# RWKV-7 scan on one core: initial states centred once ahead of the scan, and the copies of the masked product moved to ScalarE

## The chip, the core and the metric

The kernel runs on one core of one Trainium2 chip. The metric is the device time of the whole program in microseconds. An execution of the same kernel was also recorded by the hardware profiler; all rows below come from that record. The engines are named as in the profile: PE (TensorE's matmuls), PEld (its weight loads), DVE (VectorE), ACT (ScalarE), POOL (GpSimd) and SP (SyncE, which here only issues DMAs). A small q behind a name is the engine's own sequencer.

## The reference

One layer of a hybrid backbone. Rows of 128 context tokens and 2048 latent tokens, 1024 wide, are normalised, modulated and projected once. Half of the width goes through an RWKV-7 mixer of 8 heads of 64, scanned in both directions:

```python
def step(S, inp):
    r_t, w_t, k_t, v_t, kk_t, a_t = inp
    s_kk = jnp.einsum('bdhij,bdhj->bdhi', S, kk_t)
    S = (S * w_t[..., None, :] - s_kk[..., :, None] * (kk_t * a_t)[..., None, :]
         + v_t[..., :, None] * k_t[..., None, :])
    return S, jnp.einsum('bdhij,bdhj->bdhi', S, r_t)
s_final, ys = lax.scan(step, s0.astype(f32), xs)
y = ys[:, 0] + jnp.flip(ys[:, 1], axis=1)
mean = jnp.mean(y, axis=-1, keepdims=True)
var = jnp.mean(jnp.square(y - mean), axis=-1, keepdims=True)
y = ((y - mean) * lax.rsqrt(var + GN_EPS)).reshape(b, t, A_WIDTH)
```

For the context s0 is zero, and its final states are an output; for the latent tokens s0 is a given cached state for each direction and head. The other half is a gated three-tap convolution. Both halves are gated, joined, projected again, added to the input and normalised. The mean over the 64 values of a head that the last lines take away is linear in the state, so the kernel removes it from the values and from the initial states rather than from y.

## The kernel before

Three phases follow each other: the projections and gates (`phase1`, to about 1000 us), the scan (`phase2`, about 1000 to 1560 us) and the output projection (`phase3`). Only the scan and its entry are touched.

The scan works in 17 stages. A stage is a pair of heads p (0 to 3) and a block of 512 latent tokens (0 to 3), so p changes every four stages; one more stage, the sixteenth, does the context for all heads. Each stage has two groups, direction 0 and direction 1, and a group has 8 chunks (units) of 64 tokens. A chunk becomes matrix work:

- `partL` loads the operands rr of a stage, `partM` builds from them, three stages ahead (LA = 3), the block-diagonal bd (ACT), the masked products F and GA (matmuls psF and psG, masks by DVE at L893), the transposed Q (ACT), and writes the blocks dg to memory (scr_at, L897 to L899).
- `partI` solves the triangular systems of a stage on POOL: it loads ab, runs a long row of small operations (L931, L934) and writes zt to memory (scr_zt, L935).
- `partW` fills the two operand rings stl and str of the next stage: parts come by DMA (`load_stk`, L843 and L846), parts are copies from GA (`copy("g", ...)`, L950) and from Q (`copy("h", ...)`, L952). It also loads the values into the upper half of sv (`load_v`, L822) and zc from scr_zt (L959).
- `partU` transposes zc to zr (DVE, L965) and builds the operand zb (matmuls psU and psW, ACT copies to bu and zb). `partB` computes psX, which ACT puts into stl or str (L777), and psE, which DVE masks into E (L1011).
- `partS` walks the 8 chunks in order: psS is E times sv; its lower half, scaled by DVE (L1063), is the state in the lower half of the next chunk's sv. At the first chunk of a direction, for each p, the state is loaded from the input st0 into sv (L1042), and DVE takes away its mean with three operations on mn and sv (L1044 to L1046). In the context stage the state is set to zero by POOL instead.
- `finish` normalises y (yss, y) and writes it.

The helper `copy` (L772 to L779) chooses the engine: a copy goes to DVE when its letter is in `ON_DVE`, which holds the letter g alone, and to ACT otherwise. All plain copies therefore have line L779, on both engines, and are told apart by their tiles. The order of instructions on each engine comes from a scheduler that plays the whole program through with modelled costs; each engine then runs its row in that order, and an instruction that waits holds all that stand behind it on the same engine. DMAs are issued by SP, except scr_at (ACT) and scr_zt (POOL).

Of the kernel before, what the change touches and what calls it, by code (L numbers as in the profile page):

```python
# [6 lines left out]
F32 = mybir.dt.float32  # L7
# [3 lines left out]
ALU = mybir.AluOpType  # L11
# [668 lines left out]

NST = 17
MORD = ("Ff", "GgD", "", "Q")
ON_DVE = "g"
LA = 3


# [4 lines left out]
def phase2(K):  # L691
    nc, tc, A, S = K.nc, K.tc, K.A, K.S
    V, G, P, T = nc.vector, nc.gpsimd, nc.scalar, nc.tensor
    D = nc.sync.dma_start
    MF, MG, ME = (0, 1), (0, 1), (2, 3)
    B = Ctx()
    O = Ctx()
    O.scaled = None

    def setup_first():  # L700

        O.r0 = Pool(K, "p2r0", "right")
        O.rI = Pool(K, "p2rI", "right")
        O.r1 = Pool(K, "p2r1", "right")
        O.pm = Pool(K, "p2m", "right", 2, PSUM)
        B.msk = O.r0.tile([128, 4, 128], F32, name="msk")
        B.mkg = O.r0.tile([128, 2, 128], F32, name="mkg")
        for i, j in enumerate((0, 2, 4, 5)):
            D(B.msk[:, i], A["msk"][:, j, 0:128])
        for i, j in enumerate((1, 3)):  # L710
            D(B.mkg[:, i], A["msk"][:, j, 64:192])
        B.I2 = O.r0.tile([128, 64], F32, name="I2")
        D(B.I2[:], A["i2"])
        B.idt = O.r0.tile([128, 128], F32, name="idt2")
# [45 lines left out]
    def ring(pool, n, shape, name, init=None):  # L760
        l = [pool.tile(shape, F32, name=f"{name}{i}") for i in range(n)]
        if init:
            for t_ in l:
                init(t_)
        st = [0]

        def get():
            st[0] += 1
            return l[(st[0] - 1) % n]
        return get  # L770

    def copy(k, dst, src, negate=False):  # L772
        if negate:
            if k in ON_DVE:
                V.tensor_scalar(dst, src, -1.0, None, ALU.mult)
            else:
                P.activation(dst, src, AF.Copy, scale=-1.0)  # L777
        else:
            (V.tensor_copy if k in ON_DVE else P.copy)(dst, src)  # L779

# [15 lines left out]
    def tl(shape, tag, b, pool=None, dt=F32):  # L796
        return (pool or O.l0).tile(shape, dt, tag=tag, name=f"{tag}_{K.u()}", bufs=b)
# [21 lines left out]
    def load_v(dst, units):  # L819
        if units[0][0] == units[-1][0]:  # L820
            p, c0 = units[0]
            D(dst.rearrange("t u h v -> t u (h v)"), S["vt"][c0 * 64:(c0 + 8) * 64, p * 128:(p + 1) * 128].rearrange("(u t) c -> t u c", t=64))  # L822
        else:
            for u in range(2):
                D(dst.rearrange("t (g u) h v -> t u g (h v)", u=2)[:, u], S["vt"][u * 64:u * 64 + 64, :].rearrange("t (g c) -> t g c", g=4))
# [22 lines left out]
    def half(g, n):  # L848

        h = n if g.d == 0 else 1 - n  # L850
        return slice(h * 4, h * 4 + 4)
# [57 lines left out]
    def partI(s, st):  # L909
# [24 lines left out]
                G.tensor_tensor(zt[:, :kn, j + 2:32], zt[:, :kn, j + 2:32], tv[:, :, r], ALU.subtract)  # L934
        G.dma_start(S["zt"][s].rearrange("h u s b q i -> (h u s b) (q i)"), zf)  # L935

    def partW(s, st):

        for g in st.g:
            g.lt, g.rt = B.lt(), B.rt()  # L940
            g.fs, g.gs = (g.lt, g.rt) if g.d == 0 else (g.rt, g.lt)
            g.E = []
        for n in range(2):
            for g in st.g:
                us = half(g, n)
                load_stk(g.fs, g, 2, us)
                load_stk(g.gs, g, 1, us)
                for i in range(2):
                    r = slice(64 - i * 64, 128 - i * 64)
                    copy("g", g.gs[64:128, 1, i, us], g.GA[r, us, 0:64])  # L950
                    k = us.start // 2
                    copy("h", g.gs[64:128, 0, :, us.start + i:us.stop:2], g.Q[i * 64:i * 64 + 64, k:k + 2].rearrange("p k (h c) -> p h k c", h=2))  # L952
                if n == 0:
                    g.sv = tl([128, 8, 2, 64], "sv", 4)
                    load_v(g.sv[64:128], g.units)
            if n == 0:
                st.zc = tl([128, 16, 32], "zc", 1, O.l1)
                for h in range(2):
                    D(st.zc[h:128:2], S["zt"][s][h].rearrange("u s b q i -> (s b q) u i"))  # L959
            yield  # L960
# [54 lines left out]
    def partS(s, st, nxt):  # L1015

        sp = {}
        for i in range(8):
            for gi, g in enumerate(st.g):
                d = g.d  # L1020
                ctx = g.blk is None
                u = i % 4 * 2 + i // 4 if ctx else i
                u = u if d == 0 else 7 - u
                p, c = g.units[u]
                if ctx:
                    first = c == (0 if d == 0 else 1)
                    lastc = not first
                else:
                    first = c == (2 if d == 0 else 33)
                    lastc = c == (33 if d == 0 else 2)  # L1030
                sv = g.sv
                n, k = (u // 4 if d == 0 else 1 - u // 4), u % 4

                m, q = (u % 2, u // 2) if ctx else (u // 4, u % 4)
                if i == 0 and not ctx and gi in held:
                    G.tensor_copy(sv[0:64, u], held.pop(gi)[:])
                if first:
                    if ctx:
                        G.memset(sv[0:64, u], 0.0)
                    else:  # L1040
                        x = sv[0:64, u]
                        D(x, A["st0"][:, d, 2 * p:2 * p + 2, :])  # L1042
                        mn = tl([64, 2], "mn", 2)
                        V.tensor_reduce(mn[:], x, mybir.AxisListType.X, ALU.add)  # L1044
                        V.tensor_scalar(mn[:], mn[:], -1.0 / 64, None, ALU.mult)
                        V.tensor_tensor(x, x, mn[:].unsqueeze(2).broadcast_to((64, 2, 64)), ALU.add)  # L1046
                if i % 4 == 0:
                    sp[gi] = O.pS.tile([128, 4, 2, 64], F32, tag="S", name=f"psS{s}_{gi}_{i}")
                for hd in range(2):
                    T.matmul(sp[gi][:, q, hd, :], g.E[n][:, k, hd, :], sv[:, u, hd, :], start=True, stop=True)  # L1050
                if not (lastc and not ctx):
                    if ctx and lastc:
                        so = tl([64, 2, 64], "so", 2)
                        dst = so[:]
                    elif (not ctx) and i == 7:
                        if nxt.g[gi].blk is None:
                            held[gi] = tl([64, 2, 64], "held", 2)
                            dst = held[gi][:]
                        else:
                            dst = nxt.g[gi].sv[0:64, 0 if d == 0 else 7]  # L1060
                    else:
                        dst = sv[0:64, u + (1 if d == 0 else -1)]
                    r = V.tensor_tensor(dst, sp[gi][0:64, q], B.pc[0:64, d, 2 * p:2 * p + 2, c:c + 1].broadcast_to((64, 2, 64)), ALU.mult)  # L1063
                    O.scaled = r.ins
                    if ctx and lastc:
                        D(S["nst"][:, d, 2 * p:2 * p + 2, :], so[:])
                if i % 4 == 3:
                    outputs(g.units[0][0], g.blk, m, sp[gi])
            yield
# [74 lines left out]
    def first(s):  # L1144
        sts[s] = partL(s)
        yield from partM(s, sts[s])
        partI(s, sts[s])

    def early():
        setup_first()  # L1150
        for s in range(2):
            yield from first(s)

    def main():
# [64 lines left out]
        for p in (O.l0, O.rI, O.r0):  # L1219
            p.close()  # L1220

    K.early, K.main, K.spare = early, main, spare


# [14 lines left out]
    return dict(st0=st0, msk=m, i2=i2, idt=np.eye(128, dtype=np.float32))  # L1239


SCR2 = dict(at=(NST, 16, 2, 2, 32, 32), zt=(NST, 2, 16, 2, 2, 16, 32), nst=(64, 2, 8, 64))

# [128 lines left out]
def build(nc, tc, A, outs):  # L1372
# [9 lines left out]
    K.S = dict(outs)  # L1382
    for name, shape in {**SCR, **SCR2, "gate": (2, 1024)}.items():
        if name not in K.S:
# [24 lines left out]
```

## Time and profile before

| what | value |
|---|---|
| median of 3 runs | 1766.98 us (1766.21 to 1769.92) |
| the profiled execution | 1765.65 us |
| its span in the profile | 1763.5 us |
| TensorE busy in the span | 1638.5 us, 93% |
| VectorE busy | 1163.8 us, 66% |
| ScalarE busy | 815.3 us, 46% |
| GpSimd busy | 585.4 us, 33% |

The shares are means over three phases. A row of the timeline gives the start, the busy time, the engine, the line, the operation with the tiles that it writes and reads, how many instructions are merged, and in square brackets how long the engine stood idle before it and what released it. A row of waits gives the total, the number of times and the longest. A row of a group gives the busy time, the mean of one instruction in ns and the idle time before it. A row of forms gives the shortest, the median and the longest duration in ns.

### The profile page before, as it was taken

Reading aid. Unit: us, or ns where it says so; the run is one execution under the profiler, and the core shown is the slowest. Engines: PE = TensorE matmul, PEld = TensorE weight load, DVE = VectorE, ACT = ScalarE, POOL = GpSimd, SP = SyncE. Lnnn points to the kernel's source line nnn. Section 1 sums busy time; section 2 is a strip of 40 time slices with the busy share of each in tenths; the row PEclk is TensorE's granted clock in tenths of the full one; section 3 lists DMA queues with packets and bytes.
Section 4 is the critical chain, followed back from the end, with each engine's and each line's share of the span. In section 5 each row is a group of like instructions: output and inputs, shape, how many; then the busy total and the mean of one; then the engine's idle time right before and its main releaser. Section 6 shows DMA issues by size and latency. Waiting matters only on the chain. (4 is left out here: it accounts for less than half of the span.)

```text
span 1763.5 us, 33040 instructions
## 1 busy us (share of the span) xinstructions
PE 1638.5 (93%) x12400; PEld 1544.7 (88%) x12400; DVE 1163.8 (66%) x2249; ACT 815.3 (46%) x1583; POOL 585.4 (33%) x1089
## 2 busy tenths in 40 slices
PE   5999999998999998999999789899799899899998
PEld 2888889898999998999999789899799899887786
DVE  6875788866466866556773666677677777656333
ACT  4533455434144433334342367567577576533222
POOL 0011111101011111011120777767777868323221
PEclk8999999999999999999999899899999999899999
DMA  9787778785456646567767566667766875645442
GB/s 364 208 234 217 232 251 256 227 251 145 151 147 228 171 149 168 173 212 233 222 196 255 135 168 170 151 162 182 187 161 185 187 181 128 180 158 193 152 143 90
DMA packets 315664, 335.15 MB, mean 190 GB/s; under 512 B 166953, under 2 KB 263849, under 8 KB 301425
## 3 DMA queue, kind: packets, MB, share of 16 engines
q1 hardware_dynamic: 243200, 323.99, 61.5%
q10 hardware_dynamic: 70944, 4.60, 2.8%
q0 software_dynamic: 1360, 4.46, 0.7%
q8 instruction: 98, 1.61, 0.4%
q14 instruction: 62, 0.50, 0.1%
HBM read 221.16 MB, written 111.82 MB: 189 GB/s over the span
## 5 line engine op out<-in xcount | busy, mean ns | idle before, releaser
L934 POOL TENSOR_TENSOR zt<-zt,ztmp 128x30 f32<-128x30 f32 (+7 forms) x510 | 199.0, 390 | 39.1
L1010 PE MATMUL psE<-str,stl 128*128 128x128 f32 x1088 | 147.4, 280 | 13.0 <-DVE E L1011 11.1
L1050 PE MATMUL psS<-sv,E 128*128 128x64 f32 x1088 | 154.6, 274 | 2.0 <-DVE sv L1063 1.9
L1050 PEld LDWEIGHTS psS<-sv,E 128*128 128x128 f32 x1088 | 144.5, 198 | 5.2 <-DVE sv L1063 3.0
L1010 PEld LDWEIGHTS psE<-str,stl 128*128 128x128 f32 x1088 | 132.2, 193 | 15.4 <-DVE E L1011 12.0
L931 POOL TENSOR_TENSOR ztmp<-ab,zt 128x60 f32<-128x60 f32 (+7 forms) x255 | 133.1, 522 | 19.3
L779 ACT COPY bd<-rr 64x512 f32<-64x512 f32 x136 | 83.9, 617 | 84.1 <-issue 27.2
L323 POOL TENSOR_TENSOR shk<-rawl 128x384 f32<-128x384 f32 (+1 forms) x24 | 22.1, 920 | 292.3 <-ACT rawl L319 292.3
L1011 DVE TENSOR_TENSOR E<-psE,msk 128x512 f32<-128x512 f32 x136 | 93.2, 686 | 30.2 <-PE psE L1010 28.1
L1063 DVE TENSOR_TENSOR sv<-psS,pc 64x128 f32<-64x128 f32 x254 | 68.0, 277 | 42.1 <-PE psS L1050 40.4
L999 PE MATMUL psX<-F,zb 128*128 128x128 f32 x544 | 77.7, 295 | 18.5 <-DVE E L1011 17.1
L999 PEld LDWEIGHTS psX<-F,zb 128*128 128x128 f32 x544 | 70.5, 206 | 21.6 <-DVE E L1011 20.0
L892 PE MATMUL psF<-rr,bd 128*128 128x128 f32 x544 | 79.0, 291 | 9.9 <-DMA rr<-scr_ops 3.9
L1345 POOL TENSOR_TENSOR z<-z,x 128x512 f32<-128x512 f32 x32 | 43.6, 1366 | 129.1 <-DVE z L1341 107.1
L892 PE MATMUL psG<-rr,bd 128*128 128x128 f32 x544 | 73.9, 282 | 10.1 <-DVE F L893 10.1
L197 POOL TENSOR_TENSOR hslb<-kd,hshb 128x384 fp32r<-128x384 f32 (+1 forms) x24 | 26.0, 1084 | 163.7 <-ACT hshb L196 157.6
L892 PEld LDWEIGHTS psF<-rr,bd 128*128 128x128 f32 x544 | 70.3, 202 | 11.4 <-issue 6.1
L160 PE MATMUL mmc<-h,w 128*128 128x384 f32 (+1 forms) x192 | 67.5, 352 | 13.3 <-ACT q1r L321 9.7
L892 PEld LDWEIGHTS psG<-rr,bd 128*128 128x128 f32 x544 | 67.6, 196 | 10.4 <-DVE F L893 10.3
L323 POOL TENSOR_TENSOR shv<-rawl 128x384 f32<-128x384 f32 (+1 forms) x24 | 21.3, 888 | 151.9 <-ACT rawl L319 146.5
L893 DVE TENSOR_TENSOR F<-psF,msk 128x512 f32<-128x512 f32 x68 | 46.4, 683 | 30.4 <-PE psF L892 16.5
L162 PE MATMUL mmc<-h,w 128*128 128x384 f32 (+1 forms) x192 | 66.0, 344 | 0.0
(307 smaller groups left out, 5230.4 us busy)
## 6 DMA issues: line engine op xcount, KB each, us to landing
w<-scr_wsp SPq DMA_DIRECT2D x68, 1024.0 KB, 7.0
scr_wsp<-w SPq DMA_DIRECT2D x34, 1024.0 KB, 5.9
rr<-scr_ops SPq DMA_DIRECT2D x64, 512.0 KB, 4.8
scr_ops<-sp SPq DMA_DIRECT2D x160, 192.0 KB, 5.3
wr<-in_win SPq DMA_DIRECT2D x34, 512.0 KB, 6.3
ab<-scr_at SPq DMA_DIRECT2D x34, 256.0 KB, 4.1
x<-in_x SPq DMA_DIRECT2D x17, 512.0 KB, 3.8
wadas<-in_wada SPq DMA_DIRECT2D x8, 1024.0 KB, 13.0
```

What stands on the lines that cost most here:

```text
L160: T.matmul(ps[:, :n], w[:, 0, k], hh[:, 0, k, :n], start=k == 0, stop=False)
L162: T.matmul(ps[:, :n], w[:, 1, k], hh[:, 0, k, :n], start=False, stop=k == 7)
L779: (V.tensor_copy if k in ON_DVE else P.copy)(dst, src)
L892: T.matmul(ps[:, i, :].rearrange("p (a b) -> p a b", b=64), w[:, u, :], x[:, :, u, :], start=True, stop=True)
L893: V.tensor_tensor(dst[:, h * 4:h * 4 + 4, :], ps[:], mask.unsqueeze(1).broadcast_to((128, 4, 128)), ALU.mult)
L931: G.tensor_tensor(tv, ab[:, j:j + 2, j + 2:32].unsqueeze(1).broadcast_to((128, kn, 2, n)), zt[:, :kn, j:j + 2].unsqueeze(3).broadcast_to(( ...
L934: G.tensor_tensor(zt[:, :kn, j + 2:32], zt[:, :kn, j + 2:32], tv[:, :, r], ALU.subtract)
L999: T.matmul(px[:, i, :], B.zb[:, gi, us.start + i, :], g.F[:, us.start + i, :], start=True, stop=True)
L1010: T.matmul(pe[:, i, hd, :].rearrange("p (b t) -> p b t", b=2), g.lt[:, :, hd, us.start + k + i].rearrange("p b t -> p (b t)"), g.rt[:, :, ...
L1011: V.tensor_tensor(g.E[n][:, k:k + 2].rearrange("p a b c -> p (a b) c"), pe[:].rearrange("p a b c -> p (a b) c"), B.msk[:, ME[g.d]].unsquee ...
L1050: T.matmul(sp[gi][:, q, hd, :], g.E[n][:, k, hd, :], sv[:, u, hd, :], start=True, stop=True)
L1063: r = V.tensor_tensor(dst, sp[gi][0:64, q], B.pc[0:64, d, 2 * p:2 * p + 2, c:c + 1].broadcast_to((64, 2, 64)), ALU.mult)
```

## The change

The letter g leaves `ON_DVE`, so the copies of GA into stl and str, two for each half and direction of a stage, 136 of 64 x 256 in all, are made by ScalarE. The initial states of both directions and all heads are loaded once, ahead of the first stages' preparation (`center_states`, called in `early`), freed of their means by three operations of VectorE over 64 x 1024, and stored to a scratch in memory, sti. The eight loads of states into sv then read this scratch, and are issued by `partW`, directly behind the load of the values (`first_states`); `partS` no longer loads or centres. The context stage's zeros are set in `first_states` too.

```diff
--- before.py
+++ after.py
-ON_DVE = "g"
+ON_DVE = ""
...
+    def first_states(g):
+
+        for u, (p, c) in enumerate(g.units):
+            if g.blk is None and c == g.d:
+                G.memset(g.sv[0:64, u], 0.0)
+            elif g.blk is not None and c == (2 if g.d == 0 else 33):
+                D(g.sv[0:64, u], S["sti"][:, g.d, 2 * p:2 * p + 2, :])
+
+    def center_states():
+
+        x = O.rI.tile([64, 16, 64], F32, tag="ab", name="st0", bufs=2)
+        D(x[:], A["st0"].rearrange("k d h v -> k (d h) v"))
+        mn = O.rI.tile([64, 16], F32, tag="dgp", name="st0mean", bufs=1)
+        V.tensor_reduce(mn[:], x[:], mybir.AxisListType.X, ALU.add)
+        V.tensor_scalar(mn[:], mn[:], -1.0 / 64, None, ALU.mult)
+        V.tensor_tensor(x[:], x[:], mn[:].unsqueeze(2).broadcast_to((64, 16, 64)), ALU.add)
+        D(S["sti"].rearrange("k d h v -> k (d h) v"), x[:])
...
@@ partW
                 if n == 0:
                     g.sv = tl([128, 8, 2, 64], "sv", 4)
                     load_v(g.sv[64:128], g.units)
+                    first_states(g)
...
@@ partS
-                if ctx:
-                    first = c == (0 if d == 0 else 1)
-                    lastc = not first
-                else:
-                    first = c == (2 if d == 0 else 33)
-                    lastc = c == (33 if d == 0 else 2)
+                lastc = c == ((1 if d == 0 else 0) if ctx else (33 if d == 0 else 2))
...
-                if first:
-                    if ctx:
-                        G.memset(sv[0:64, u], 0.0)
-                    else:
-                        x = sv[0:64, u]
-                        D(x, A["st0"][:, d, 2 * p:2 * p + 2, :])
-                        mn = tl([64, 2], "mn", 2)
-                        V.tensor_reduce(mn[:], x, mybir.AxisListType.X, ALU.add)
-                        V.tensor_scalar(mn[:], mn[:], -1.0 / 64, None, ALU.mult)
-                        V.tensor_tensor(x, x, mn[:].unsqueeze(2).broadcast_to((64, 2, 64)), ALU.add)
...
@@ early
         setup_first()
+        center_states()
...
+SCR2: sti=(64, 2, 8, 64)
```

The scheduler orders the program anew. Instructions on PE and POOL are as many as before, DVE has 157 fewer, ACT has 136 more, and SP has two more. In the new file the masking of E is at L1030, the state's scaling at L1067, y at L1084, zr at L984 and the load of zc at L978. Late in phase 1, where PE waits for the first rr near 934 us, SP's row now has the load of the states ahead of the four loads of rr, and PE's row has eight mmgb matmuls ahead of the first psF.

The first place is VectorE's row at the start of the scan, behind the setup of the rings; F and GA are the masked products of stage 2, whose psF and psG run at that time. Before:

```order
L794 COPY str_10032<-I_9259 64x512 x2
L794 COPY str_10033<-I_9259 64x512 x2
L779 COPY str_10032<-GA_9266 64x256 x2
L779 COPY stl_10027<-GA_9269 64x4x64 x2
L893 TENSOR_TENSOR F_10011<-psF_0_0_10070,msk 128x512
L893 TENSOR_TENSOR F_10011<-psF_0_1_10076,msk 128x512
L779 COPY str_10032<-GA_9266 64x256 x2
L779 COPY stl_10027<-GA_9269 64x4x64 x2
L893 TENSOR_TENSOR GA_10012<-psG_0_0_10082,mkg 128x512
```

and after:

```order
L794 COPY str_10040<-I_9260 64x512 x2
L794 COPY str_10041<-I_9260 64x512 x2
L893 TENSOR_TENSOR F_10019<-psF_0_0_10080,msk 128x512
L893 TENSOR_TENSOR F_10019<-psF_0_1_10086,msk 128x512
L893 TENSOR_TENSOR GA_10020<-psG_0_0_10092,mkg 128x512
L893 TENSOR_TENSOR GA_10020<-psG_0_1_10098,mkg 128x512
L984 STREAM_TRANSPOSE zr_10215<-zc_10069 128x512
```

The eight copies from GA are gone from between the presets, F and GA; in ScalarE's row 16 copies, from GA and Q in turn, now stand in one piece, ahead of the next bd.

The second place is VectorE's row where stage 8 begins, the first stage of the third pair of heads (its E's, and GA of a later stage, are made there; yss and y_12550 belong to `finish`). Before:

```order
L1114 TENSOR_REDUCE yss_13276<-w_13260 128x8
L1011 TENSOR_TENSOR E_13026<-psE_0_00_13042,msk 128x512
L1063 TENSOR_TENSOR sv_12753<-psS_1_4_13008,pc 64x128
L1080 TENSOR_TENSOR y_12545<-psS_1_4_13008,y_12545 64x512
L1117 RECIPROCAL yss_13276<-yss_13276 128x8
L1044 TENSOR_REDUCE mn_13623<-sv_13150 64x2
L1011 TENSOR_TENSOR E_13034<-psE_1_00_13048,msk 128x512
L1118 TENSOR_TENSOR y_12550<-y_12550,yss_13276 128x512
L893 TENSOR_TENSOR GA_9272<-psG_0_1_13248,mkg 128x512
L1045 TENSOR_SCALAR mn_13623<-mn_13623 64x2
```

and after:

```order
L1118 TENSOR_REDUCE yss_13270<-w_13254 128x8
L1030 TENSOR_TENSOR E_13018<-psE_0_00_13034,msk 128x512
L1067 TENSOR_TENSOR sv_12745<-psS_1_4_13000,pc 64x128
L1084 TENSOR_TENSOR y_12537<-psS_1_4_13000,y_12537 64x512
L1121 RECIPROCAL yss_13270<-yss_13270 128x8
L1030 TENSOR_TENSOR E_13026<-psE_1_00_13040,msk 128x512
L1122 TENSOR_TENSOR y_12542<-y_12542,yss_13270 128x512
L893 TENSOR_TENSOR GA_9273<-psG_0_1_13242,mkg 128x512
L1030 TENSOR_TENSOR E_13018<-psE_0_01_13046,msk 128x512
L1067 TENSOR_TENSOR sv_12736<-psS_0_0_13212,pc 64x128
```

The operations on mn and sv of L1044 and L1045 are gone from between the reciprocal, the E's and y, as are the copies into str that followed; nothing here reads what a load brings into sv's lower half.

The third place is SP's row ahead of stage 3, where zc is loaded in two halves. Before:

```order
L822 DMA sv_11128<-scr_vt 64x8x128
L822 DMA sv_11137<-scr_vt 64x8x128
L868 DMA rr_9281<-scr_ops_57 128x2x512
L959 DMA zc_11139<-scr_zt 64x16x32
L846 DMA stl_10026<-scr_ops_57 64x4x64 x2
L843 DMA str_10032<-scr_ops_57 64x2x256
L843 DMA str_10033<-scr_ops_59 64x2x256
L846 DMA stl_10027<-scr_ops_59 64x4x64 x2
L959 DMA zc_11139<-scr_zt 64x16x32
```

and after:

```order
L822 DMA sv_11128<-scr_vt 64x8x128
L822 DMA sv_11137<-scr_vt 64x8x128
L978 DMA zc_11139<-scr_zt 64x16x32 x2
L846 DMA stl_10034<-scr_ops_57 64x4x64 x2
L843 DMA str_10040<-scr_ops_57 64x2x256
L843 DMA str_10041<-scr_ops_59 64x2x256
L846 DMA stl_10035<-scr_ops_59 64x4x64 x2
```

The second half of zc stood behind six loads of operands and now directly follows the first.

More of the change, by code (lines that the diff above doesn't have):

```diff
@@ L1239, in layout2 @@
     return dict(st0=st0, msk=m, i2=i2, idt=np.eye(128, dtype=np.float32))
-SCR2 = dict(at=(NST, 16, 2, 2, 32, 32), zt=(NST, 2, 16, 2, 2, 16, 32), nst=(64, 2, 8, 64))
+SCR2 = dict(at=(NST, 16, 2, 2, 32, 32), zt=(NST, 2, 16, 2, 2, 16, 32), nst=(64, 2, 8, 64), sti=(64, 2, 8, 64))
 def phase3(K):
```

## The prediction

> **What bounds the kernel now.** I read the page first, then busy time by stretches of the scan, then the waits of TensorE and VectorE, and last the timeline where a wait was long. Head of the page:
>
> ```profile
> span 1763.5 us, 33040 instructions
> PE 1638.5 (93%) x12400; PEld 1544.7 (88%) x12400; DVE 1163.8 (66%) x2249; ACT 815.3 (46%) x1583; POOL 585.4 (33%) x1089
> ```
>
> TensorE is the bound as a mean over stages, but the change touches the scan alone (about 1000 to 1560 us), so its share is to be read there. Each row is a stretch: its length, busy us of TensorE, of its weight loads, of VectorE, ScalarE and POOL (instructions in brackets), then TensorE's granted clock, the DMA share and GB/s:
>
> ```profile
> 1000.00:1050.00 50.00, 34.81 (x374) 33.20 (x373) 35.29 (x64) 29.31 (x54) 40.32 (x88) 0.86 0.67 167
> 1200.00:1250.00 50.00, 48.92 (x593) 47.93 (x592) 39.89 (x84) 37.34 (x70) 39.37 (x88) 1.00 0.78 189
> 1250.00:1300.00 50.00, 42.24 (x520) 41.49 (x519) 33.65 (x76) 27.98 (x52) 32.22 (x73) 0.93 0.67 170
> ```
>
> In a regular stretch (1200) TensorE is 98% busy at full clock: little to win there. In two others it is not: the start of the scan loses some 15 us, and 1250 to 1300 loses 8, with the clock below 1. What TensorE waits for from 1000 to 1600 us (total, times, longest):
>
> ```profile
> PE psX L999 <- DVE E L1011: 17.1, 14, 5.9
> PE psE L1010 <- DVE E L1011: 11.1, 6, 7.4
> PE psG L892 <- DVE F L893: 10.1, 1, 10.1
> PE psF L892 <- ACT Q L779: 3.5, 3, 2.7
> PE psE L1010 <- ACT stl L777: 1.7, 2, 1.3
> PE psX L999 <- ACT zb L777: 1.3, 1, 1.3
> PE psW L980 <- ACT bu L779: 1.2, 2, 0.7
> ```
>
> Some 38 us hang on VectorE, not quite 8 on ScalarE. VectorE in turn is held, in order, by one wait that the change removes:
>
> ```profile
> DVE mn L1044 <- DMA sv<-in_st: 17.1, 6, 7.7
> ```
>
> **The change, part by part.** (a) The initial states. At a change of head pair the mean's reduction stands in VectorE's row ahead of E, and its load is issued only then:
>
> ```profile
> 1265.71 0.52 SPq L1042 DMA_DIRECT2D sv<-in_st  x1
> 1269.90 0.28 DVE L1044 TENSOR_REDUCE mn<-sv 64x2 f32<-64x128 f32 x1 [7.69 <-DMA sv<-in_st]
> 1258.98 1.06 PE L1010 MATMUL psE<-str,stl 128*128 128x128 f32 x8
> 1259.87 0.56 PE L1050 MATMUL psS<-sv,E 128*128 128x64 f32 x4
> 1270.96 2.08 PE L1010 MATMUL psE<-str,stl 128*128 128x128 f32 x8 [7.40 <-DVE E L1011]
> 1272.82 0.95 PE L1050 MATMUL psS<-sv,E 128*128 128x64 f32 x4
> 1401.98 2.08 PE L999 MATMUL psX<-F,zb 128*128 128x128 f32 x8 [5.86 <-DVE E L1011]
> 1403.85 0.95 PE L1050 MATMUL psS<-sv,E 128*128 128x64 f32 x4
> 1404.60 2.02 PE L892 MATMUL psF<-rr,bd 128*128 128x128 f32 x8
> 1406.41 1.58 PE L999 MATMUL psX<-F,zb 128*128 128x128 f32 x8
> ```
>
> VectorE stands still for 7.69 us, TensorE for 7.40, and its first matmuls then run slow: 2.08 against 1.06 us for eight, 0.95 against 0.56 for four, 1.41 us in all. After the change VectorE's row holds no operation on sv here (second place of the order), and the state is wanted only by psS, whose loads now stand beside load_v in SP's queue, ahead of the stage. What is late next is the ordinary wait of psX on E: by the table above (17.1 - 5.86) / 13 = 0.86 us. First stall: 7.40 + 1.41 - 0.86 = 7.95. Second, at 1401.98: 5.86, and slow matmuls of 1.02 and 0.39 again, and, by the same pace of 1.06 for eight, 0.96 and 0.52 more, 2.89 in all; less 0.86: 7.89. Together 15.8; as bounds, nothing if another input is just as late (POOL's result, below), and 17.6 if the 0.86 goes too. What is left of VectorE's 17.1 us after these two stalls I count as nothing: it lies at the start of the scan and in stage 3, where (b) and (d) hold TensorE longer.
>
> What else this part moves: SP issues the eight state loads as before, now from scratch and directly behind load_v, which waits for the same buffer of sv; the scratch is written late in phase 1, so no new wait stands ahead of the loads of operands that follow. The context stage's eight memsets on POOL come earlier in its row and stay eight. Nothing for both; if the state loads should hold SP's queue, each holds it for its 0.52 us, 4.2 in all.
>
> (b) Start of the scan.
>
> ```profile
> 1004.51 0.59 DVE L779 COPY str<-GA 64x256 f32<-64x256 f32 x2
> 1005.12 5.62 DVE L779 COPY stl<-GA 64x256 f32<-64x256 f32 x2
> 1010.76 1.29 DVE L893 TENSOR_TENSOR F<-psF,msk 128x512 f32<-128x512 f32 x2
> 1011.51 3.68 PE L892 MATMUL psG<-rr,bd 128*128 128x128 f32 x16 [10.15 <-DVE F L893]
> 1011.81 2.50 ACT L779 COPY zb<-zc 32x512 f32<-32x512 f32 x4 [5.79 <-POOL zt L934]
> ```
>
> Four copies, of which two took 5.62 us, stand ahead of F, and TensorE waits 10.15 us for F. In the changed row F stands directly behind the presets of L794, so it could start at 1004.51: 6.25 us sooner. But zc comes no sooner than the 1011.81 at which ScalarE's zb starts, and if all waits on zc the gain is nothing. Between 0 and 6.25 I take 3.5, a little over half, because the psG that stood still needs F and not zc. ScalarE gets 16 copies in a row here, in the 5.79 us in which it was idle and a little of what lies before.
>
> (c) Late in phase 1. The row of TensorE now has eight mmgb matmuls ahead of the first psF, and SP's has center_states's load ahead of the four rr loads:
>
> ```profile
> 939.32 3.25 PE L892 MATMUL psF<-rr,bd 128*128 128x128 f32 x16 [3.95 <-DMA rr<-scr_ops]
> 944.13 0.33 PE L161 MATMUL mmgb<-h,w 128*128 128x384 f32 x1
> 944.30 0.33 PE L162 MATMUL mmgb<-h,w 128*128 128x384 f32 x1
> ```
>
> Eight at a spacing of 0.17 us fill 1.4 of the 3.95; the added load delays rr by about its issue, 0.6 us as the 0.52 above, or by more if the transfer is in the way (2.4 makes it a loss of 1). Taken: +0.8, between -1 and 1.4. The three centring operations (VectorE is 66% busy) and the store lie in this same gap, long before 1000 us: nothing; without that cover, three at 0.7 us.
>
> (d) Stage 3. The two zc loads stand apart in SP's row, with six operand loads between them, and everybody waits for the second one:
>
> ```profile
> 1104.14 0.60 SPq L959 DMA_DIRECT2D zc<-scr_zt  x1
> 1108.80 0.61 SPq L959 DMA_DIRECT2D zc<-scr_zt  x1
> 1111.60 0.71 DVE L965 STREAM_TRANSPOSE zr<-zc 128x512 f32<-128x512 f32 x1 [3.57 <-DMA zc<-scr_zt]
> ```
>
> In the new row they stand together (third place of the order): the second could go 4.66 - 0.6 = 4.1 us sooner, and VectorE's 3.57 us with it. Bounds: 0, if the POOL result is what sets it, and 9 with the stretch of slow clock behind it. Taken: 4.
>
> (e) The copies on VectorE.
>
> ```profile
> L779 ACT COPY str<-Q x68: 401/403/408, 1002.7 to 1532.2; 64x256 f32<-64x256 f32 x68
> L779 DVE COPY str<-GA x68: 286/343/1534, 1004.5 to 1531.8; 64x256 f32<-64x256 f32 x68
> L779 DVE COPY stl<-GA x68: 285/321/3547, 1005.1 to 1533.9; 64x256 f32<-64x256 f32 x68
> L779 DVE COPY stl<-GA 64x256 f32<-64x256 f32 x68 | 33.2, 488 | 1.6
> L779 DVE COPY str<-GA 64x256 f32<-64x256 f32 x68 | 31.4, 462 | 2.4 <-PE psE L1010 0.4
> ```
>
> VectorE sheds 33.2 + 31.4 = 64.6 us, ScalarE gets 136 x 0.403 = 54.8 us, 3.2 us a stage, in rows where it is 56 to 75% busy. Where the copies stand between two E's, E comes sooner. The waits on E without the two stalls are 17.1 - 5.86 + 11.1 - 7.40 = 14.9 us, of which 3 belong to the stage of (d): 11.9. Half of it, 6, is taken, since the E's also wait for psE; bounds 0 and 11.9.
>
> The Trainium skill speaks against this part: "ScalarE: Activation LUTs", section "Rules for kernel authors", has simple elementwise work go to VectorE, which is up to about three times faster there. The smallest times above (285 against 403) agree in sign, the means (488 and 462 against 403) do not: priced by the smallest, the move would add 136 x 0.12 = 16 us of work; by the means it saves 10.
>
> (f) ScalarE's side. The same copies now stand in its row ahead of zb, bu, Q and stl. TensorE's waits on it are 3.5 + 1.7 + 1.3 + 1.2 = 7.7 us. I let them grow by half, -3.7; bounds: 0, and -28 if 2 of the 3.2 us a stage come through in 14 regular stages.
>
> Sum: 15.8 + 3.5 + 0.8 + 4 + 6 - 3.7 = 26.4 us. The profiled execution took 1765.65 us (span 1763.5, the rest lies around it): 1739.25. The median of the runs is 1766.98, 1.33 more: 1740.6.
>
> **The rivals.** Part of it comes back: at the places of (a) and (d) a second input is nearly as late. For it: POOL is busy 39.37 of 50 us in the regular stretch, and in (b) and (d) ScalarE and VectorE do wait for its result or for zc. Against it: in 17 stages VectorE waited for zc only twice, and one of these is (d):
>
> ```profile
> DVE zr L965 <- DMA zc<-scr_zt: 4.2, 2, 3.6
> ```
>
> The gain is then one stall's worth and a little, 10 us: 1757.
>
> ScalarE becomes the bound, which ends on the other side. Its row is in order; if the new copies delay stl or zb, and so psE and psX, by 2.5 us in each of 14 stages, 35 us are lost against the 30.1 of the other terms: 5 us slower, 1772. It decides from 30.1 / 14 = 2.15 us a stage on. For it: in the row at 1200 it had 12.7 us in 50 free, 7.6 a stage, in pieces. Against it: it needs 3.2 of the 7.6, and TensorE waits for it 7.7 us in the whole scan. The rule of the Trainium skill on ScalarE quoted above, taken alone, points to this case.
>
> VectorE's waits vanish wholly: (e) gives 11.9, (b) 6.25, (d) 9, and (f) nothing: 15.8 + 6.25 + 0.8 + 9 + 11.9 = 43.8, or 1723; with (d) at the 4 of the sum, 38.8 and so 1728, which I take for it. For it: the copies' spread from 285 to 3547 ns while POOL works beside them, so that POOL too may gain when they leave. The Trainium skill has a reason, "SBUF — State Buffer", section "Terms": VectorE and GpSimd lock a port pair against each other, and ScalarE has its own. The 3547 ns copy, with POOL busy beside it, agrees; by that rule POOL's chain shortens too.
>
> The edit does nothing for the time: only if TensorE's 98% stretch were the whole story, which the 8 us stalls speak against.
>
> **How the numbers follow.** Forecast as summed, 1740.6: 0.45, its own range 1733 to 1750. Partly given back, 1757: 0.25. Waits vanish, 1728: 0.15. ScalarE the bound, 1772: 0.09. No change: 0.05. The last 0.01 is for what I have not thought of. A difference under 0.2% (3.5 us) cannot be told from none. Range 1726 to 1760: below it lies the part of the third case that goes to 1723, above it the last two and the upper edge of the second. Faster 0.86, same 0.05, slower 0.09.
>
> **What would show it.** Right: no VectorE wait on an sv load; TensorE's waits on E before the stages with new states under 2 us; stretch 1250 to 1300 over 46 us busy; psG's wait for F near 5; VectorE's busy time down by some 70 us and ScalarE's up by 55. Wrong: TensorE's waits on stl, zb, bu or Q growing beyond 15 us, zb or zr waiting for zc or POOL longer than before, or new waits of psS on sv<-scr_sti.

## The result, and the profile after

The changed kernel takes 1749.28 us in the median of four runs (1741.7 to 1754.7), the kernel before 1768.22 (1766.21 to 1769.92). The ratio is 0.9893, with a 95% interval of 0.987 to 0.9916: 19 us faster, where 26 were forecast. Two more comparisons on other chips gave 0.9915 (0.9885 to 0.9945) and 0.9903 (0.9868 to 0.9939). The profiled execution was one of the slower ones, at 1754.7 us. Its page begins:

```profile
span 1752.9 us, 33041 instructions
PE 1647.9 (94%) x12400; PEld 1558.8 (89%) x12400; DVE 1093.0 (62%) x2092; ACT 870.1 (50%) x1719; POOL 582.1 (33%) x1089
```

VectorE is 70.8 us less busy and ScalarE 54.8 us more, as forecast. The same stretches as before (columns as above), and what TensorE waits for in the scan:

```profile
1000.00:1050.00 50.00, 38.47 (x413) 36.26 (x412) 23.53 (x46) 32.34 (x65) 41.36 (x92) 0.97 0.76 182
1200.00:1250.00 50.00, 47.98 (x485) 46.55 (x484) 30.55 (x61) 38.28 (x73) 38.81 (x90) 0.90 0.75 177
1250.00:1300.00 50.00, 49.81 (x651) 48.81 (x650) 36.33 (x75) 39.48 (x78) 35.99 (x84) 1.00 0.76 199
```

```profile
PE psF L892 <- ACT Q L779: 9.8, 22, 1.6
PE psE L1029 <- DVE E L1030: 7.0, 4, 3.5
PE psG L892 <- DVE F L893: 4.4, 2, 4.0
PE psE L1029 <- ACT stl L777: 4.0, 4, 1.9
PE psU L992 <- DVE zr L984: 2.8, 1, 2.8
PE psX L1018 <- ACT zb L777: 2.3, 2, 1.7
```

The stretch of the old stall (1250 to 1300) is now full: 49.81 of 50 us at full clock. But 1200 to 1250, which had been full at clock 1.00, is now at 0.90. The waits on E are down from 28.2 to 7.8 us; those on ScalarE are up from 7.7 to 17.4 (with 0.7 on bu and 0.6 on bd). The row of VectorE waiting for a load of sv is gone, and another has grown:

```profile
DVE zr L984 <- DMA zc<-scr_zt: 13.9, 4, 4.8
```

Where the clock fell, in a stage with no wait over 1.5 us, TensorE's timeline reads:

```profile
1216.60 1.06 PE L892 MATMUL psF<-rr,bd 128*128 128x128 f32 x8
1217.59 1.20 PE L992 MATMUL psU<-zr,GA 32*32 32x32 f32 x64
1218.72 1.10 PE L1054 MATMUL psS<-sv,E 128*128 128x64 f32 x8
1221.28 2.08 PE L892 MATMUL psF<-rr,bd 128*128 128x128 f32 x8 [1.46 <-ACT Q L779]
1228.92 3.24 PE L1018 MATMUL psX<-F,zb 128*128 128x128 f32 x16
```

A wait of 1.46 us for Q, and for about 10 us from then on eight psF take 2.08 instead of 1.06 us, sixteen psX 3.24 instead of 1.95. The wait itself is small; the stretch at half clock behind it costs about 5 us.

For each run below the scan was split in the same way: from the first psF behind the last mmb to the end of the last psS; TensorE's idle time in it; and, in pieces of 2 us, what the granted clock lacks to 1. The rest is work at full clock. All in us, one profiled execution each:

| kernel | scan | idle | lost to the clock | rest |
|---|---|---|---|---|
| before | 598.7 | 54.0 | 25.6 | 519.1 |
| changed | 586.4 | 36.2 | 27.4 | 522.8 |
| changed, second profile | 573.2 | 29.8 | 20.5 | 522.9 |
| changed, third profile | 580.3 | 34.5 | 23.9 | 521.9 |
| states only | 585.3 | 44.7 | 20.5 | 520.1 |
| copies only | 592.6 | 42.5 | 30.7 | 519.4 |

Three executions of one program differ by 13 us in the scan, and about half of that is clock. Their mean is 580.0, 18.7 us under the kernel before: by these columns idle time is 20.5 less, clock loss 1.7 less and the rest 3.4 more. But the columns overlap where TensorE stands still at half clock: 5.8 us in the kernel before, in its three long waits, and 0.2 to 0.8 in the three. Counted once, as idle time, the clock's loss is 19.8 us before and 23.4 in the mean after, and the rest is 1.8 less. The kernel before has a single profile here. Over whole executions, the span times what the mean granted clock lacks to 1 is 55.9 us in the mean of 17 executions before and 56.5 in six of the changed kernel on one chip, 56.8 (11) and 58.6 (six) on another. The stalls went away, the lost clock did not.

### The profile page after: what moved, and what is told of

Read it like the earlier page. It is cut to its first block, busy times and chain, and to the rows that moved or that the text cites. A ratio compares the mean times of both kernels' runs of the same rounds, so it can differ in the third digit from the quotient of the medians.

```text
span 1752.9 us, 33041 instructions
## 1 busy us (share of the span) xinstructions
PE 1647.9 (94%) x12400; PEld 1558.8 (89%) x12400; DVE 1093.0 (62%) x2092; ACT 870.1 (50%) x1719; POOL 582.1 (33%) x1089
## 5 line engine op out<-in xcount | busy, mean ns | idle before, releaser
L1067 DVE TENSOR_TENSOR sv<-psS,pc 64x128 f32<-64x128 f32 x254 | 69.2, 277 | 92.9 <-PE psS L1054 92.2
L1030 DVE TENSOR_TENSOR E<-psE,msk 128x512 f32<-128x512 f32 x136 | 92.7, 684 | 33.0 <-PE psE L1029 32.3
L160 PE MATMUL mmc<-h,w 128*128 128x384 f32 (+1 forms) x192 | 67.9, 354 | 13.4 <-ACT q1r L321 9.8
L323 POOL TENSOR_TENSOR shv<-rawl 128x384 f32<-128x384 f32 (+1 forms) x24 | 25.4, 1060 | 153.4 <-ACT rawl L319 153.4
L892 PEld LDWEIGHTS psG<-rr,bd 128*128 128x128 f32 x544 | 65.7, 193 | 5.0 <-DVE F L893 4.8
L161 PE MATMUL mmc<-h,w 128*128 128x384 f32 (+1 forms) x192 | 66.1, 344 | 0.0
L162 PE MATMUL mmc<-h,w 128*128 128x384 f32 (+1 forms) x192 | 65.7, 342 | 0.0
```

The lines of the kernel that those rows point to most:

```text
L160: T.matmul(ps[:, :n], w[:, 0, k], hh[:, 0, k, :n], start=k == 0, stop=False)
L161: T.matmul(ps[:, :n], w[:, 0, k], hh[:, 1, k, :n], start=False, stop=False)
L162: T.matmul(ps[:, :n], w[:, 1, k], hh[:, 0, k, :n], start=False, stop=k == 7)
L892: T.matmul(ps[:, i, :].rearrange("p (a b) -> p a b", b=64), w[:, u, :], x[:, :, u, :], start=True, stop=True)
L1030: V.tensor_tensor(g.E[n][:, k:k + 2].rearrange("p a b c -> p (a b) c"), pe[:].rearrange("p a b c -> p (a b) c"), B.msk[:, ME[g.d]].unsquee ...
```

## The experiments

**The same kernel again.** No edit.

> The changed kernel once more, unaltered. Theory C (half-clock stretches): its times so far lie at 1741.7, 1744.3, 1754.3 and 1754.7 us, because TensorE's granted clock falls to 0.50 for some 10 us at places with short waits, not at the same places in every execution. Expected: times again spread over more than 5 us (the kernel before over less than 4), and a profile whose stretches at 0.50 lie in part at other places than 1056, 1124 and 1220 us. Rival (one fixed schedule, and the spread is a matter of the chip): times within 4 us, stretches at the same places.

Ratio 0.9915; times from 1748.7 to 1767.1, a spread of 18 us (before 1768.3 to 1781.3, 13 us, on the same chip). Two stretches at half clock of 10.2 us begin at 1127.9 and 1223.5 us (1125.7 and 1221.3 in the first profile), one of 10.2 us at 1057.4 has become one of 3.4 us at 1056.3, and the loss fell by 6.9 us. Most places recur, their length and some of them do not; the spread of before was larger than the theory said, so the comparison of spreads decides little.

**The states alone.** `ON_DVE` goes back:

```diff
-ON_DVE = ""
+ON_DVE = "g"
```

> Only the initial states are changed; the copies of GA stay on VectorE. Theory A (the states' stalls carry the gain): 14 to 18 us faster than before, TensorE waits 17.1 and 11.1 us for E fall by 13 together, no wait of VectorE for a load of sv. Rival B (the copies carry it, the stalls are refilled by the next input): under 6 us faster.

Ratio 0.9932 (0.9906 to 0.9957), that is 12 us of 1774, with an interval of 7.6 to 16.7 us. The profile has no wait of VectorE on a load of sv, and TensorE's waits on E are 8.5 and 8.2 us, 11.5 less. A little under theory A's 14 and over B's 6: the initial states carry most of the gain. One new wait has appeared, of psE for str on ScalarE (8.5 us in all, 6.3 the longest); what causes it was not followed.

**The copies alone.** In the kernel before:

```diff
-ON_DVE = "g"
+ON_DVE = ""
```

> Only the copies of GA move to ScalarE; the initial states are loaded and centred in the scan as before. Theory A: the stalls at the two changes of heads (7.40 and 5.86 us) stay, the time is within 5 us of before, since what E gains is lost to psF waiting for Q on ScalarE. Rival B: 8 us or more faster.

Ratio 0.9978 (0.9963 to 0.9993), 4 us. The stall on the states stays:

```profile
PE psE L1010 <- DVE E L1011: 14.1, 4, 6.2
PE psF L892 <- ACT Q L779: 9.1, 18, 2.1
PE psX L999 <- ACT zb L777: 6.1, 4, 1.7
DVE mn L1044 <- DMA sv<-in_st: 13.7, 3, 6.5
```

The small waits on E are replaced by small waits on Q and zb. By the table idle time falls by 11.5 us and the clock loss grows by 5.1. Theory A as expected; the two parts, 12 and 4 us, come to about the 15 of the whole on that chip. The order of the DMAs changed here too: the two loads of zc stand together ahead of stage 3, as in the changed kernel, while in the run with the states alone they stand 4.7 us apart.

**Q's copy on VectorE.**

```diff
-ON_DVE = ""
+ON_DVE = "q"
```

> The changed kernel, with the 34 copies of Q out of PSUM made by VectorE instead of ScalarE. Theory D (ScalarE's row became too long ahead of Q: TensorE waits 9.8 us in 22 places for Q, and some of these waits set off the stretches at half clock): the waits for Q fall under 3 us, fewer stretches at 0.50 in the regular stages, time 5 to 12 us under the changed kernel's. Rival (these waits are noise, TensorE is bound elsewhere): within 3 us of the changed kernel.

Ratio 0.9916 (0.989 to 0.9942), no better than the changed kernel, and theory D fell in this form. The waits for Q are gone, and others stand there:

```profile
PE psW L999 <- ACT bu L779: 5.9, 7, 1.9
PE psE L1029 <- ACT stl L777: 5.6, 3, 4.3
PE psS L1054 <- DVE sv L1067: 4.9, 3, 3.1
```

The scan had 33.5 us of idle time and 35.8 of lost clock, the most of all runs, and over its six whole executions the clock's loss is 64.4 us in the mean, against the changed kernel's 56.5 on that chip. The short waits that replaced those for Q did no less harm.

**Reference for the next three.** The changed kernel again.

> The changed kernel a third time, as the measure for the three beside it on the same chip. Theory C: a third pattern of half-clock stretches; time 1 to 1.5% under the kernel before.

Ratio 0.9903 (0.9868 to 0.9939); the longer stretches at half clock begin at 1065, 1133, 1229 and 1498 us, loss 23.9.

**The centring later.**

```diff
         setup_first()
-        center_states()
-        for s in range(2):
-            yield from first(s)
+        f = first(0)
+        next(f)
+        yield
+        center_states()
+        yield from f
+        yield from first(1)
```

> The changed kernel, with the load of the states and its centring placed behind the four first loads of rr instead of ahead of them. Theory E (the load ahead of rr puts the entry of the scan off by 3 to 4 us; POOL's row of solves starts that much later, and zc with it, which paces the first stages): the wait of psF for rr falls from 5.9 to about 4, the scan starts 2 to 4 us sooner, zr's waits for zc in the first stages shrink, time 3 to 5 us under the changed kernel's. Rival (the entry is made up for in the scan, which POOL or TensorE bounds anyway): within 1.5 us.

Ratio 0.9897 (0.9866 to 0.9928), 1 us from the reference: not to be told apart from it. In the profile the place itself did change. Rows of before, of the changed kernel and of this one:

```profile
933.98 1.91 SPq L868 DMA_DIRECT2D rr<-scr_ops  x4
```

```profile
935.38 0.52 SPq L948 DMA_DIRECT2D st<-in_st  x1
936.08 1.99 SPq L868 DMA_DIRECT2D rr<-scr_ops  x4
943.16 3.75 PE L892 MATMUL psF<-rr,bd 128*128 128x128 f32 x16 [5.88 <-DMA rr<-scr_ops]
```

```profile
944.24 1.91 SPq L868 DMA_DIRECT2D rr<-scr_ops  x4
949.59 3.56 PE L892 MATMUL psF<-rr,bd 128*128 128x128 f32 x16 [4.26 <-ACT bd L779]
```

From SP's first load to psF it took 5.3 us before, 7.8 with the states ahead and 5.35 with them behind. That is 2 to 2.4 us for one load of 0.52 us of issue; whether the transfers share a way or something else makes up the rest was not tried. The local price is shown; the scan starts at 1009.7 us in this run and at 1009.6 in the reference, so no later start of the scan can be put down to it, and its worth in the whole time, if any, is under what the runs tell.

**Extra matmuls ahead of psU.**

```diff
+        fl = pu[:].rearrange("p u i -> p (u i)")
+        for k in range(8):
+            T.matmul(fl[:, k % 4 * 128:k % 4 * 128 + 128], st.g[0].GA[:, k, :], st.g[0].F[:, k, :], start=True, stop=True)
```

> The changed kernel, with eight more matmuls of 128x128 ahead of each stage's psU, written into the same PSUM tile and overwritten by psU; they add nothing to the result and cost TensorE about 17 x 8 x 0.12 = 16 us. Theory C (the clock falls where a few microseconds hold little matrix work: the 32x32 matmuls of psU and psW together with a wait of about 1 us): fewer stretches at 0.50 in the regular stages, their loss in the scan falls from 20 to 27 us to under 15, and the time grows by clearly less than 16 us, or falls. Rival (waits alone set the stretches off): as much loss as before, and the time 12 us or more longer than the changed kernel's.

A product is two instructions here, so 272 were added, 1.95 us a stage and 33 us in all, twice what the expectation says. Ratio 0.9919 (0.9888 to 0.995): 3 us more than the reference. Busy time of TensorE and its clock over 1080 to 1500 us, of the changed kernel and of this one:

```profile
1080.00:1500.00 420.00, 406.45 (x4903) 395.36 (x4902) 264.29 (x546) 331.91 (x635) 320.04 (x721) 0.97 0.71 172
```

```profile
1080.00:1500.00 420.00, 417.55 (x5115) 409.38 (x5116) 264.99 (x549) 336.46 (x644) 326.89 (x733) 1.00 0.73 175
```

```profile
1220.54 1.95 PE L991 MATMUL psU<-F,GA 128*128 128x128 f32 x16
1222.42 1.20 PE L995 MATMUL psU<-zr,GA 32*32 32x32 f32 x64
1223.55 1.10 PE L1057 MATMUL psS<-sv,E 128*128 128x64 f32 x8
1224.49 1.11 PE L892 MATMUL psF<-rr,bd 128*128 128x128 f32 x8
```

Not one stretch at half clock is left in these 420 us. In the scan the clock loss is 15.3 (under 15 was expected) and the idle time 22.7 us. All six executions have a mean granted clock of 0.974 to 0.978, those of the reference 0.960 to 0.971, which makes 15.5 us less lost. So most of 33 us of useless work was paid by waits and clock that it prevented. Neither of the rival's signs came. But the filling covers the waits for Q too (2.2 us left in these 420, none over 0.3), so this run alone does not tell missing work from waits; the last section takes that up from the windows of all traces.

**Two, and four, instead of eight.** `range(2)` and `range(4)` in the same place.

> The changed kernel with two extra matrix products ahead of each stage's psU, overwritten by psU. One product is two matmul instructions in the trace (16 stood there for eight products, 1.95 us a stage), so this adds 17 x 4 x 0.12 = 8 us of work. Theory C: a smaller filling prevents only some of the half-clock stretches between 1075 and 1500 us, and 4 to 8 us of waits and lost clock come back; time within 4 us of the changed kernel's. Rival (any additional matmul keeps the clock up): no stretch there at all and 6 us or more faster.

> As the run with two, with four extra products a stage: 16 us of added work. Theory C: stretches at half clock between 1075 and 1500 us nearly gone, as with eight; 8 to 16 us of waits and lost clock come back, time 0 to 6 us under the changed kernel's. Rival (only the whole length of eight fills the gap): stretches as without filling, time 8 us or more longer.

Ratios 0.9974 (0.9956 to 0.9992) and 0.9933 (0.9912 to 0.9954), against 0.9893 to 0.9915 of the changed kernel: the first clearly slower than it, the second slower with intervals that overlap. With four, one long stretch and one short are left in 1080 to 1500, the scan's loss is 18.8 and its idle time 27.6 us; the time was forecast wrongly. With two the profile shows more lost than with none, 34.1 us, and 38.9 idle, and no theory here expected the slower time:

```profile
1080.00:1500.00 420.00, 407.40 (x4792) 397.00 (x4791) 264.60 (x535) 328.95 (x630) 321.87 (x725) 0.96 0.74 174
```

This profile is of the slowest of its 12 executions. Over all 12 the mean granted clock is 0.967, as over the reference's six, so two products did not raise the clock, and that they lower it is not shown. Every such edit also reorders the rows of all engines, so the series is no clean measure of the amount. Only the end with eight is clear; what made the run with two slower than the changed kernel stays open.

**Half of the copies back.**

```diff
-                    copy("g", g.gs[64:128, 1, i, us], g.GA[r, us, 0:64])
+                    copy("gG"[i], g.gs[64:128, 1, i, us], g.GA[r, us, 0:64])
```

with `ON_DVE = "G"`.

> The changed kernel with every second copy of GA (68 of 136) back on VectorE. Theory D in its weaker form (the sum of short waits on E and on Q counts, whoever causes them): waits for Q fall to about half of 9.8 us, waits for E stay under 10, idle time of TensorE in the scan 30 us or less, time 0 to 6 us under the changed kernel's. Rival: VectorE's waits come back (over 15 us) and the time goes up by 3 us or more.

Ratio 0.9907 (0.9873 to 0.9942), as the reference. Q's waits fell to 3.6 us, but stl's rose to 11.4 (one of 8.1); idle time 37.5 us against the 30 expected.

**POOL's solves cut short.** The triangular solve is left unfinished in the first four stages:

```diff
-        for m in range(15):
+        for m in range(8 if s < 4 else 15):
```

> The changed kernel with POOL's solve cut to 8 of its 15 steps in the first four stages; the inverse is left unfinished there. Theory F (POOL's solves pace the first four stages: zr waits 13.9 us for zc in four places, and the copies taken off VectorE could not bring these stages forward): zr's waits for zc under 3 us, the scan 6 to 12 us shorter than the changed kernel's. Rival (these stages are paced by TensorE or ScalarE, zc is only next in line): under 3 us.

```profile
DVE zr L984 <- DMA zc<-scr_zt: 1.8, 1, 1.8
```

The waits for zc are gone but for 1.8 us. Ratio 0.9876 (0.9846 to 0.9906), about 5 us under the 0.990 that the changed kernel's three comparisons average to, with intervals that overlap. The scan took 572.5 us, which the changed kernel's second profile also reaches (573.2), so the whole does not decide. The stages do. From the scan's start the first four zr come at 13.7, 34.0, 65.7 and 95.6 us; in the three profiles of the changed kernel they come at 13.7 to 14.2, 45.3 to 45.5, 76.3 to 79.6 and 106.3 to 110.2. So theory F holds from the second stage on, by 11 to 15 us that are mostly lost again later, and not for the first zr.

**Two edits for a faster version.** The late centring, and psQ first:

```diff
-MORD = ("Ff", "GgD", "", "Q")
+MORD = ("Q", "Ff", "GgD", "")
```

> The changed kernel with two edits: the load of the states behind the first loads of rr (it took 2 us out of the entry of the scan), and psQ first among the pieces of a stage's preparation, so that the copy of Q on ScalarE has longer until psF needs its PSUM buffer. Theory: waits of psF for Q fall from about 10 to under 5 us and with them some stretches at half clock; time 3 to 8 us under the changed kernel's, a ratio to before near 0.986. Rival: the waits move to bu, zb or stl, as they did when VectorE copied Q; a ratio of 0.989 to 0.992 as the changed kernel's.

Ratio 0.9938 (0.9917 to 0.9959): slower in the middle than all three comparisons of the changed kernel, with an interval that overlaps theirs. The waits for Q fell to 4.4 us, and zb took their place:

```profile
PE psX L1018 <- ACT zb L777: 13.8, 12, 2.8
PE psF L892 <- ACT Q L779: 4.4, 10, 2.3
```

The rival was right on the waits, and the time was above both. No complete version tried here is shown to beat the changed kernel.

## Why the prediction was right, and where its sizes were off

The direction, the range and the main cause held; the point, 1740.6 us, was 8.7 too low. Part of this is luck. The measured time lies as near to the first rival's 1757 as to the point, and that rival's reason, a second input nearly as late, held at (b) and in part at (d). All that the prediction named as signs of being right came, but so did two of its three signs of being wrong: zr waits longer for zc (13.9 us against 4.2), and the waits on ScalarE passed 15.

The two separate runs split the sum. The states alone stand for (a) and (c), forecast at 16.6 us, and give 12 (7.6 to 16.7). The copies alone stand for (b), (d), (e) and (f), forecast at 9.8, and give 4 (1.2 to 6.6): there the prediction was too high. By its terms:

(a) The two stalls, 15.8 us: shown. The states alone give 12 us, and that includes the loss at (c); their scan is 13.4 us shorter. No wait of VectorE on a load of sv is left, the stretch from 1250 is full, and of the half clock behind the two stalls (6.8 us each, from 1267.5 and 1400.7) nothing is left: none of the three profiles of the changed kernel has any between 1240 and 1465 us.

(b) Start of the scan, 3.5 us: the mechanism was right, psG's longest wait for F fell from 10.15 to 3.99 us. The size was not: from the start of the scan to the first zr it took 14.9 us before (1014.28 - 999.42) and takes 14.2 now (13.7 and 14.2 in the other two profiles). The bound that the prediction named, zc, came true:

```profile
1008.92 0.76 POOL L935 DMA_DIRECT2D scr_zt<-zt  x1 [0.31 <-POOL zt L934]
1012.03 1.32 SPq L978 DMA_DIRECT2D zc<-scr_zt  x2
1016.66 0.71 DVE L984 STREAM_TRANSPOSE zr<-zc 128x512 f32<-128x512 f32 x1 [4.79 <-DMA zc<-scr_zt]
1017.43 0.81 PE L992 MATMUL psU<-zr,GA 32*32 32x32 f32 x38 [2.79 <-DVE zr L984]
```

POOL's store goes out at 1008.92, zc is loaded at 1012.03, zr starts when it has landed, at 1016.66, and what VectorE no longer does it waits. POOL alone is not what holds this: with the short solves its store goes out 5.0 us ahead of the scan's start instead of 6.4 behind it, and the first zr still comes 13.7 us after that start. There zc is issued in one go behind SP's other loads.

(d) Stage 3, 4 us: the mechanism was right, and its lower bound took most of the gain. The second zc load went out beside the first, and VectorE still waits:

```profile
1101.59 0.20 POOL L923 COPY dgp<-ab 128x16 f32<-128x16 f32 x1 [7.65 <-DMA ab<-scr_at]
1104.40 0.60 POOL L935 DMA_DIRECT2D scr_zt<-zt  x1 [0.30 <-POOL zt L934]
1108.53 1.31 SPq L978 DMA_DIRECT2D zc<-scr_zt  x2
1112.67 0.71 DVE L984 STREAM_TRANSPOSE zr<-zc 128x512 f32<-128x512 f32 x1 [3.64 <-DMA zc<-scr_zt]
```

3.64 us, as 3.57 before. SP's order did cost what the prediction said. From POOL's store to zr it took 12.7 us before and 11.6 with the states alone, where the two loads stand apart, and 8.1 to 8.4 in the three profiles of the changed kernel. But the store itself, counted from the scan's start, came at 101.9, 98.2 and 101.7 us, against 99.5 before: in the two late cases POOL had stood 7.65 and 7.79 us waiting for its own input ab, in the other 2.52, and 2.95 before. What made ab late was not followed. So from the scan's start to this zr (b) and (d) together brought 2.0, 5.9 and 2.1 us of the 7.5 (112.2 us before; 110.2, 106.3 and 110.1 after).

(c) The entry, +0.8 us: wrong sign at its place. The wait of psF for rr grew from 3.95 to 5.88 us, and the states' load ahead of rr costs 2 to 2.4 us, beyond the lower bound of -1. Whether the scan starts later for it is not shown: in the three profiles of the changed kernel it starts at 1002.5, 1009.2 and 1009.6 us, and with the load behind rr at 1009.7.

(e) The small waits on E: 14.9 us were left after the stalls, of which 6 were to go. By the table of waits 7.8 remain, so 7 went. As a sum of waits that is about right; as time, part of it was given back at (f).

(f) ScalarE's side: -3.7 us forecast; its waits grew by 9.7 us, past the 15 in all that the prediction had set as the sign of a miss. Term mis-sized by 6 us in waits alone. And the prediction's sum took each new wait at its length. The runs show that in these stages a wait of 1 to 1.5 us can carry another 5 us of half clock with it. (a) reckoned 4.3 us of slow matmuls behind the old stalls as won; they are gone there, and come back elsewhere: counted once, the clock's loss in the scan is 3.5 us more in the mean than in the one profile before.

ScalarE did not become the bound: the copies alone, without the states, still gain 4 us. The moved copies take 396 to 405 ns there. The factor of three that the prediction quotes from the Trainium skill ("ScalarE: Activation LUTs", section "Rules for kernel authors") is given there for bf16, and these copies are fp32. The rival of waits vanishing wholly did not come either. Its reason, that POOL gains when the copies leave VectorE, can be read: the mean of POOL's two solve operations over the scan went from 389 and 517 ns to

```profile
L934 POOL TENSOR_TENSOR zt<-zt,ztmp 128x120 f32<-128x120 f32 (+7 forms) x492 | 189.6, 385 | 37.9
L931 POOL TENSOR_TENSOR ztmp<-ab,zt 128x220 f32<-128x220 f32 (+7 forms) x245 | 125.5, 512 | 18.4
```

that is by 1%. The lock between VectorE and GpSimd that the Trainium skill describes ("SBUF — State Buffer", section "Terms") agrees with the longest VectorE copy, 3547 ns with POOL busy beside it, though no run isolates it; for POOL's chain the leaving of the copies was worth nearly nothing.

## What to carry to other kernels

A load that is issued just ahead of its use, with an in-order engine waiting for it, is worth removing: here it held two engines for 7 us, most of that length came back as time, and it was found in one row of the waits. Moving work from one busy in-order engine to another mostly moves the short waits; count those that will appear on the receiving engine, in front of which consumer, before counting those that vanish. And where the start of a pipeline waits for the load of a third engine's result, freeing the other two brings little there (0.7 to 1.2 us of 3.5).

## What the runs showed of the hardware

At two places of the changed kernel the granted clock fell to half although TensorE had not been idle for more than 1.6 us at a time. The stretches at 1125.7 and 1221.3 us both stand behind 64 matmuls of 32x32 in 1.2 us, eight of 128x64 and waits of 1.5 to 2.3 us in all, and last 10.2 us; in other executions of the same program similar stretches begin some microseconds earlier or later, are shorter, or fail to come. With sixteen full matmuls (1.95 us) ahead of the small ones the clock stayed at 1.00 for 420 us.

The 14 profiles of this case say more. The granted clock is 1.00 or 0.50 in all of them, nothing between. All 106 stretches at 0.50 that begin within the scan last one to five times 3.41 us, and within one execution all of them begin on one grid of that spacing, to within 2 ns. So the traces can be cut into windows of this grid. Let each window be weighed by its matmul instructions: the columns that each streams, times its share of the 128x128 array, so that a 32x32 matmul counts a sixteenth of its columns. A window at full clock has 3264 such columns in the median. Of the 61 windows at full clock with fewer than 1000, 60 were followed by half clock; of 131 with 1000 to 1600, 44; of 1989 with more, two. Of 82 windows at half clock with fewer than 1400, 80 were followed by another one; of 122 with more, 18.

So the fall follows a window short of matrix work, and a window may be short without any wait. Two windows of the third profile of the changed kernel, and the one behind them (columns as in the prediction):

```profile
1491.73:1495.14 3.41, 3.41 (x33) 3.34 (x31) 2.88 (x6) 3.04 (x7) 2.94 (x7) 1.00 0.25 62
1495.14:1498.55 3.41, 3.41 (x109) 3.20 (x110) 2.00 (x6) 2.45 (x6) 2.94 (x7) 1.00 0.40 102
1498.55:1501.96 3.41, 3.41 (x56) 3.35 (x48) 1.03 (x2) 1.17 (x2) 2.94 (x7) 0.50 0.19 46
```

TensorE is busy through the whole second window, with small matmuls for the most part (960 weighed columns), and the clock falls behind it. This speaks for theory C against its rival of the run with eight products: a fall needs no wait, and a wait counts as one of the ways in which a window comes short of work. It also fits the places that move: where the grid lies against the program differs from one execution to the next. Where between 1000 and 1600 the limit lies was not found.

The Trainium skill ("TensorE: Matmul & The Clock Gate", Part 1) has the clock halve after an idle window of about 3.4 us, with the window running freely. The length and the free running agree with the grid of 3.41 us. That the window must be idle does not: of the 106 falls only 10 stand behind a window with TensorE busy for less than 2% of it, and 48 behind one with more than half.
